# Attention on one core: the transposes of a step's two heads side by side, the gate steps between them moved to the fillings around

## The chip, the core and the metric

The kernel runs on one core of a Trainium2 chip. TensorE (PE) multiplies matrices and transposes; VectorE (DVE), ScalarE (ACT) and GpSimd (POOL) work beside it on vectors; SyncE (SP) and POOL issue most of the DMAs. TensorE's results land in PSUM, eight banks of 128 x 512 float32. The metric is device time in microseconds (us), from runs of the whole kernel.

## The reference

One block of a streaming encoder on 512 tokens of width 1024: a normalised input goes through one wide projection into two branches (gated linear attention with 4 heads, and "forgetting" attention with 8 heads), each branch is projected to 1024 channels, the two are merged by sigmoid gates that come from the same projection, then an output projection, and a gated feed-forward part with a short convolution. The part that matters here is the second branch and the gates:

```python
def fox_attention(q, k, v, log_f):              # 512 tokens, 8 heads of 64
    c = jnp.cumsum(log_f, axis=1)
    for i in range(S // Q_BLOCK):               # 4 blocks of 128 queries
        lo, hi = i * Q_BLOCK, (i + 1) * Q_BLOCK
        logits = q[lo:hi] @ k[:hi].T * scale + c[lo:hi, None] - c[None, :hi]
        p = softmax(where(causal, logits, -inf))
        outs.append(p @ v[:hi])
...
y = sigmoid(g_gla + gate_b[0]) * (o_gla @ w_gla_branch) \
    + sigmoid(g_fox + gate_b[1]) * (o_fox @ w_fox_branch)
```

## The kernel before

Every float32 matrix is split into a high and a low part, and a product is taken as three matmuls (function `mm3`, lines 314 to 316). The weights come from memory in pieces of 128 x 1024: `piece()` hands out the next one and, three pieces ahead, issues its load on SP, ScalarE's cast to the high part (L277) and VectorE's difference for the low part (L278).

The attention works on pairs of heads. There are four pairs and four query blocks, so 16 steps, in the list `steps_a`; the block `qb` of a step sees `qb + 1` blocks of 128 keys. One step has three parts, and they are written in a software pipeline over a loop index `i`:

- `logits(pair, qb)` at `i`: six matmuls into two banks `lg` (L929); per head VectorE adds the forget term `cb` and takes the minimum (L934), ScalarE takes the exponential (L939), VectorE the reciprocal of the sum (L940), ScalarE scales (L941, tile `pr`).
- `transposed(h, qb)` at `i + 1`, once for each head of the pair (h = 2 pair + 0 or 1): TensorE transposes the `qb + 1` blocks of `pr` into a bank `pt` (L951), ScalarE copies out the high part `ph` (L959), VectorE takes the low part `pl` (L960). There are two banks `pt`.
- `values(h, half)` at `i + 2`, when two query blocks are there: products of `ph` and `pl` with the values into a bank `po` (L975, L976).

Between these stand pieces of other work. `work` is a list of generators, and `fill(n)` takes n steps from it. Most of them are gates: `gate_tile` (12 in this stage, for the output gate `zr` and the merge gate `zg`) makes one 128 x 512 tile in eight steps of three matmuls in a bank `ps_mm`, fetches its weight piece before the first, and after the eighth VectorE scales the tile out of the bank (L879). The others are `prepare_k` and `prepare_q`, one step each: four transposes (L891, L902) into a bank, then ScalarE's high part (L893, L904) and VectorE's low part (L894, L905) of the keys or queries of a pair. For pairs 1 to 3 that bank is also a `ps_mm`. There are two banks `ps_mm`, taken in turn, so the next tile but one waits until a tile is read out.

The list is, in order: half of gate 0, prepare_k and prepare_q of pair 0, the rest of gate 0, gate 1, prepare_k(1), the products of gate 2, prepare_q(1), gate 2's scaling, prepare_k(2), gate 3, prepare_q(2), gate 4, prepare_k(3), gate 5, prepare_q(3), and gates 6 to 11: 104 steps, of which nine are taken ahead of the loop. How many are taken in the loop stands in the table `FILL` (L41): its row is `i % 4`, so the rows go with `qb` = 0, 1, 2, 3 of the logits, and its numbers are the fillings behind the logits, behind the first head's transposes and behind the second head's.

The instructions are written in this order, and a planner then lays out each engine's queue. It goes by priorities in the order of the source and by its own estimates of when an operand or a bank is ready; where it holds an instruction for not ready, a later one can go ahead. So the order in the trace is near that of the source, but not the same everywhere. Each queue is then run in its order.

Of the kernel before, what the change touches and what calls it, by code (L numbers as in the profile page):

```python
# [20 lines left out]
NT = T // P  # L21
# [16 lines left out]
NPB = (KB + 1) // 2  # L38
NTAIL = 5
NSPARE = 4  # L40
FILL = ((3, 2, 2), (2, 2, 2), (2, 2, 1), (2, 2, 2))  # L41
QSTEP = 8
GAHEAD = 2
NWARM = 9
# [34 lines left out]
def hybrid_kernel(ctx: ExitStack, tc, xT, xt, wp, wu, wd, wf, pp, aw2, fing, out):  # L79
# [341 lines left out]
    def fill(n=1 << 30):  # L421
        while n > 0 and work:
            try:
                next(work[0])
                n -= 1
            except StopIteration:
                work.pop(0)
# [492 lines left out]
    def logits(pair, qb):  # L920

        kh, kl, qh, ql = qk[pair]
        n = (qb + 1) * P
        q = slice(qb * P, n)
        rows = [slice(i * FD, (i + 1) * FD) for i in range(2)]
        lgs = [bank("lg") for _ in range(2)]
        for j, (a, b) in enumerate(((qh, kh), (ql, kh), (qh, kl))):
            for lg, r in zip(lgs, rows):
                mm(lg[:, :n], lhsT=a[r, q], rhs=b[r, :n], start=(j == 0), stop=(j == 2))  # L929
        for i, lg in enumerate(lgs):  # L930
            h = 2 * pair + i
            pr = fpool.tile([P, T], F32, tag="pr", name="pr", bufs=4)
            nm = fpool.tile([P, 1], F32, tag="nm", name="nm", bufs=4)
            nc.vector.tensor_tensor_reduce(  # L934
                out=pr[:, :n], in0=lg[:, :n], in1=cbs.pop((h, qb)), scale=-1.0, scalar=3e38,
                op0=ALU.add, op1=ALU.min, accum_out=nm,
            )
            rs = fpool.tile([P, 1], F32, tag="rs", name="rs", bufs=4)
            nc.scalar.activation(out=pr[:, :n], in_=pr[:, :n], func=AF.Exp, scale=-1.0, bias=nm, accum_out=rs)  # L939
            nc.vector.reciprocal(out=rs, in_=rs)  # L940
            nc.scalar.activation(out=pr[:, :n], in_=pr[:, :n], func=AF.Copy, scale=rs)  # L941
            probs[h, qb] = pr
            if h + 2 < FH:
                load_cb(h + 2, qb)

    def transposed(h, qb):
        pr = probs.pop((h, qb))
        pt = bank("pt")
        for kb in range(qb + 1):
            c = slice(kb * P, (kb + 1) * P)  # L950
            nc.tensor.transpose(pt[:, c], pr[:, c], ident)  # L951
        half, odd = qb // 2, qb % 2
        if odd == 0:
            pts[h, half] = [
                fpool.tile([P, 2 * half + 2, 2 * P], F32R, tag=f"{tag}{half}", name=tag, bufs=2) for tag in ("ph", "pl")
            ]
        ph, pl = (t[:, : qb + 1, odd * P : (odd + 1) * P] for t in pts[h, half])
        pt3 = pt.rearrange("p (a q) -> p a q", q=P)[:, : qb + 1, :]
        last_copy[:] = [nc.scalar.copy(out=ph, in_=pt3)]  # L959
        nc.vector.tensor_sub(out=pl, in0=pt3, in1=ph.bitcast(F32))  # L960
# [3 lines left out]
    def values(h, half):  # L964

        ph, pl = pts.pop((h, half))
        v2 = vs[h]
        if half == 0:
            po[h] = bank("po")
        nk = 2 * half + 2  # L970
        for kb in range(nk):
            w = v2[:, kb, :, :].rearrange("p a d -> p (a d)")
            lo = P if kb == nk - 1 else 0
            q = slice(half * 2 * P + lo, (half + 1) * 2 * P)
            mm(po[h][:, q], lhsT=w, rhs=ph[:, kb, lo:], start=(kb == 0), stop=False)  # L975
            mm(po[h][:, q], lhsT=w, rhs=pl[:, kb, lo:], start=False, stop=(kb == nk - 1))  # L976
        if half == 0:
            return

        i, pair = h % 2, h // 2  # L980
        if i == 0:
            oo[pair] = fpool.tile([P, T], F32, tag="oo", name="oo", bufs=1)

        ol = fpool.tile([P, 4, 2 * P], F32, tag="ph1", name="ol", bufs=2).rearrange("p a q -> p (a q)")[:, :T]
        nc.scalar.copy(out=ol[:FD], in_=po[h][FD:P, :])
        nc.vector.tensor_add(out=oo[pair][i * FD : (i + 1) * FD, :], in0=po[h][:FD, :], in1=ol[:FD])
        if h + 2 < FH:
            prepare_v(h + 2)

    def split_values(pair):  # L990
        nc.scalar.copy(out=oth[pair], in_=oo[pair])
        nc.vector.tensor_sub(out=otl[pair], in0=oo[pair], in1=oth[pair].bitcast(F32))

    steps_a = [(pair, qb) for pair in range(FH // 2) for qb in range(NT)]
# [9 lines left out]
    for i in range(len(steps_a) + 2):  # L1004
        last = None
        if i < len(steps_a):
            logits(*steps_a[i])
            fill(FILL[i % NT][0])
        for j in range(2):
            if 0 <= i - 1 < len(steps_a):  # L1010
                transposed(2 * steps_a[i - 1][0] + j, steps_a[i - 1][1])
                fill(FILL[i % NT][1 + j])
        if i >= 2 and steps_a[i - 2][1] % 2 == 1:
            pair, qb = steps_a[i - 2]
            for j in range(2):
                values(2 * pair + j, qb // 2)

        if i > NT and i % NT == 2:
            split_values(i // NT - 1)
# [664 lines left out]
```

## Time and profile before

| what | value |
|---|---|
| median of 3 runs | 705.51 us (704.78 to 706.0) |
| the profiled execution: time | 703.98 us |
| the profiled execution: span from first to last instruction | 702.3 us |
| TensorE busy | 693.0 us (99%) |
| VectorE busy | 551.1 us (78%) |
| ScalarE busy | 426.8 us (61%) |
| GpSimd busy | 179.3 us (26%) |
| mean granted clock of TensorE | 0.999 |
| moved by DMA | 138.20 MB |

A row of the timeline has the start in us, the duration, the engine, the line of the kernel, the operation, the output and inputs, the tile's shape, and how many neighbours of a kind are merged in it; in brackets, for how long the engine was idle before and what released it. Durations of matmuls overlap, since they are pipelined: what one costs is read from its start to the next one's. "PEld" is the loading of a matmul's weights, which runs beside the matmul before it. A row of waits has the waiting engine and line, what it waited for, the total in us, the number of times and the longest; "issue" is time in which it waited for nothing that the profile shows.

### The profile page before, as it was taken

The numbers are of one execution on the slowest core, as the hardware profiler recorded it, in microseconds if no ns is written. First come the engines' busy times: TensorE is split into PE (matmuls) and PEld (weight loads), VectorE is DVE, ScalarE is ACT, GpSimd is POOL, SyncE is SP. The second block draws the span as 40 slices with busy tenths as digits, with TensorE's granted clock in tenths as the row PEclk, the third lists the DMA queues.
The fourth block names the chain that finished last, engine by engine and source line by source line (L and its number), as shares of the span: only waits on it lengthen the run. The fifth ranks groups of instructions, "written<-read, shape, count | busy, mean of one in ns | idle before, by whom it ended". The sixth has DMA issues, their size and how long they took to land.

```text
span 702.3 us, 11231 instructions
## 1 busy us (share of the span) xinstructions
PE 693.0 (99%) x4162; PEld 601.6 (86%) x4162; DVE 551.1 (78%) x836; ACT 426.8 (61%) x690; POOL 179.3 (26%) x228
## 2 busy tenths in 40 slices
PE   8999999999999999999999999999999999999996
PEld 6887788777877888888888999999999999888885
DVE  7875887876666585677769998888988889987984
ACT  7488565667676753334484965655556566655753
POOL 7215010124231323323100133322343411000222
PEclk9999999999999999999999999999999999999999
DMA  9668478996775478977885778877777787775643
GB/s 321 267 184 276 113 239 214 310 226 150 175 172 122 105 205 219 248 178 198 195 285 120 154 182 206 189 171 185 167 185 170 196 210 227 269 211 178 194 136 120
DMA packets 44743, 138.20 MB, mean 197 GB/s; under 512 B 5240, under 2 KB 8328, under 8 KB 44560
## 3 DMA queue, kind: packets, MB, share of 16 engines
q1 hardware_dynamic: 30864, 92.85, 39.4%
q0 software_dynamic: 10656, 39.33, 31.6%
q10 hardware_dynamic: 3168, 5.31, 2.1%
q8 instruction: 33, 0.54, 0.3%
q14 instruction: 22, 0.18, 0.1%
HBM read 133.25 MB, written 27.28 MB: 229 GB/s over the span
## 4 chain that ended last, share of the span: by engine, by line
PE 90%; DVE 5%; ACT 2%; DMA 1%; issue 1%; ACTq 0%; DVEq 0%; SPq 0%
PE ps_mm L314 22%; PE ps_mm L315 21%; PE ps_mm L316 21%; PE ps_ax L315 7%; PE ps_ax L316 6%; PE ps_ax L314 6%; DVE wl L278 2%; PE ps_lg L929 2%; PE ps_pt L951 1%; PE ps_po L976 1%; PE ps_po L975 1%; DMA raw<-wsum 1%; DMA ppt<-in_pp_dram 1%; DVE xo L1274 1%; PE ps_ax L832 1%
## 5 line engine op out<-in xcount | busy, mean ns | idle before, releaser
L314 PE MATMUL ps_mm<-xh,wh 128*128 128x512 f32 (+1 forms) x312 | 109.7, 353 | 1.2 <-DVE wh L273 1.2
L277 ACT CAST wh<-rawx 128x1024 fp32r<-128x1024 f32 x75 | 76.2, 1016 | 52.8 <-PE ps_mm L315 24.1
L315 PE MATMUL ps_mm<-xl,wh 128*128 128x512 f32 (+1 forms) x312 | 106.4, 341 | 0.0
L316 PE MATMUL ps_mm<-xh,wl 128*128 128x512 f32 (+1 forms) x312 | 106.3, 342 | 0.0
L278 DVE TENSOR_TENSOR wl<-rawx,wh 128x1024 fp32r<-128x1024 f32 x75 | 88.8, 1188 | 16.4 <-ACT wh L277 16.4
L278 DVE TENSOR_TENSOR wl<-raw,wh 128x1024 fp32r<-128x1024 f32 x58 | 78.3, 1351 | 9.1 <-ACT wh L277 8.2
L277 ACT CAST wh<-raw 128x1024 fp32r<-128x1024 f32 x58 | 60.7, 1048 | 34.3 <-PE ps_mm L315 24.6
L314 PEld LDWEIGHTS ps_mm<-xh,wh 128*128 128x128 f32 x312 | 58.7, 188 | 9.6 <-issue 2.8
L316 PEld LDWEIGHTS ps_mm<-xh,wl 128*128 128x128 f32 x312 | 58.6, 188 | 7.4 <-DVE wl L274 0.4
L315 PEld LDWEIGHTS ps_mm<-xl,wh 128*128 128x128 f32 x312 | 58.8, 189 | 5.6 <-DVE xl L1183 0.2
L285 POOL DMA_DIRECT2D rawx<-in_wu_dram x30 | 26.1, 869 | 124.6 <-DVE wl L278 117.7
L278 DVE TENSOR_TENSOR wl<-rawz,wh 128x1024 fp32r<-128x1024 f32 x31 | 39.2, 1266 | 14.8 <-ACT wh L277 14.1
L314 PE MATMUL ps_mm<-xo,wh 128*128 128x256 f32 x160 | 45.4, 284 | 0.0
L315 PE MATMUL ps_mm<-xo,wh 128*128 128x256 f32 x160 | 45.3, 283 | 0.0
L316 PE MATMUL ps_mm<-xo,wl 128*128 128x256 f32 x160 | 45.3, 283 | 0.0
L314 PE MATMUL ps_mm<-xc,wh 128*128 128x256 f32 (+1 forms) x128 | 43.5, 340 | 0.0
L314 PE MATMUL ps_mm<-wh,xh 128*128 128x512 f32 x108 | 42.8, 397 | 0.1
L277 ACT CAST wh<-rawz 128x1024 fp32r<-128x1024 f32 x31 | 32.5, 1047 | 16.5 <-PE ps_mm L316 6.0
L251 POOL TENSOR_TENSOR rawx<-rawx,raw 128x256 f32<-128x256 f32 x32 | 36.7, 1175 | 22.5 <-DMA rawx<-in_wu_dram 22.5
L315 PE MATMUL ps_mm<-xc,wh 128*128 128x256 f32 (+1 forms) x128 | 42.4, 332 | 0.0
L316 PE MATMUL ps_mm<-xc,wl 128*128 128x256 f32 (+1 forms) x128 | 42.3, 331 | 0.0
L315 PE MATMUL ps_mm<-wl,xh 128*128 128x512 f32 x108 | 42.1, 390 | 0.0
(477 smaller groups left out, 1986.1 us busy)
## 6 DMA issues: line engine op xcount, KB each, us to landing
rawx<-in_wu_dram POOLq DMA_DIRECT2D x32, 512.0 KB, 6.0
rawz<-in_wp_dram SPq DMA_DIRECT2D x30, 512.0 KB, 4.3
raw<-in_wp_dram SPq DMA_DIRECT2D x22, 512.0 KB, 4.4
wsum<-in_wd_dram SPq DMA_DIRECT2D x20, 512.0 KB, 6.4
rawx<-in_wu_dram SPq DMA_DIRECT2D x20, 512.0 KB, 5.5
raw<-in_wu_dram SPq DMA_DIRECT2D x20, 512.0 KB, 4.3
rawx<-wsum SPq DMA_DIRECT2D x12, 512.0 KB, 4.4
wsum<-in_wd_dram POOLq DMA_DIRECT2D x10, 512.0 KB, 7.5
```

The lines of the kernel that those rows point to most:

```text
L251: nc.gpsimd.tensor_add(out=raws[n][:, c], in0=raws[n][:, c], in1=raws[other][:, c])
L277: nc.scalar.copy(out=hi[:, :m], in_=raw[:, :m])
L278: nc.vector.tensor_sub(out=lo[:, :m], in0=raw[:, :m], in1=hi[:, :m].bitcast(F32))
L285: added[:] = [nc.gpsimd.dma_start(raw, recipes[i][0], accum_op=ALU.add)]
L314: mm(ps, lhsT=ah, rhs=bh, start=start, stop=False, **k)
L315: mm(ps, lhsT=ah, rhs=bl, start=False, stop=False, **k)
L316: mm(ps, lhsT=al, rhs=bh, start=False, stop=stop, **k)
L832: mm(obs[par][:, c], lhsT=scs[2 * u + par][:, 2 * t2 + j, :], rhs=vg[:, 2 * u + t2, h * GDV : (h + 1) * GDV], start=(t2 == j == 0), stop=F ...
L929: mm(lg[:, :n], lhsT=a[r, q], rhs=b[r, :n], start=(j == 0), stop=(j == 2))
L951: nc.tensor.transpose(pt[:, c], pr[:, c], ident)
L975: mm(po[h][:, q], lhsT=w, rhs=ph[:, kb, lo:], start=(kb == 0), stop=False)
L976: mm(po[h][:, q], lhsT=w, rhs=pl[:, kb, lo:], start=False, stop=(kb == nk - 1))
```

## The change

Only the places at which steps of `work` are taken change. The filling between the two heads' transposes is gone; its steps are divided between the filling behind the logits and the one behind both groups of transposes. The total of each row stays (7, 6, 5, 6). At `i` = 0 there are logits and no transposes, so four steps are taken there in place of three, and from there the list stands one step further on at each of the logits; at `i` = 16, where there are only transposes, the table gives three in place of two and two.

```diff
-FILL = ((3, 2, 2), (2, 2, 2), (2, 2, 1), (2, 2, 2))
+FILL = ((4, 3), (3, 3), (3, 2), (3, 3))
...
     for i in range(len(steps_a) + 2):
         last = None
         if i < len(steps_a):
             logits(*steps_a[i])
             fill(FILL[i % NT][0])
         for j in range(2):
             if 0 <= i - 1 < len(steps_a):
                 transposed(2 * steps_a[i - 1][0] + j, steps_a[i - 1][1])
-                fill(FILL[i % NT][1 + j])
+        if 0 <= i - 1 < len(steps_a):
+            fill(FILL[i % NT][1])
         if i >= 2 and steps_a[i - 2][1] % 2 == 1:
             pair, qb = steps_a[i - 2]
             for j in range(2):
                 values(2 * pair + j, qb // 2)
```

## The prediction

> **What bounds the kernel now.** I read the page first, for the span and the busy shares of the engines; then the busy time by stretch, for the stage of the change alone; then TensorE's waits in it; then its timeline row by row.
>
> ```profile
> span 702.3 us, 11231 instructions
> PE 693.0 (99%) x4162; PEld 601.6 (86%) x4162; DVE 551.1 (78%) x836; ACT 426.8 (61%) x690; POOL 179.3 (26%) x228
> ```
>
> TensorE is busy for 693.0 of 702.3 us, far ahead of VectorE's 551.1. What the kernel loses to waits of TensorE anywhere is at most 9.3 us, so the question is how much of that lies in the attention stage. That stage runs from the first logits at 136.8 us to the last values at 235 us. The view of busy time by stretch gives it next to the start and the rest:
>
> ```profile
> core 0: us, PE busy (x) PEld busy (x) DVE busy (x) ACT busy (x) POOL busy (x), PEclk, DMA share, GB/s
> 133.00:236.00 103.00, 102.96 (x585) 82.05 (x584) 67.89 (x171) 70.55 (x167) 30.07 (x57) 1.00 0.73 175
> 0.00:8.00 8.00, 5.51 (x18) 2.76 (x19) 2.87 (x8) 4.03 (x6) 4.49 (x16) 1.00 0.76 229
> ```
>
> In the stage TensorE is busy for 102.96 of 103.00 us at a granted clock of 1.00; VectorE has work for 67.89 us and ScalarE for 70.55 us. The stage's length is therefore the sum of what TensorE issues plus small waits at its weight loads, which the view of waits lists for the same stretch:
>
> ```profile
> PEld ps_lg L929 <- issue: 2.7, 8, 0.4
> PEld ps_mm L314 <- issue: 1.9, 6, 0.4
> PEld ps_lg L929 <- DVE rs L940: 0.7, 2, 0.4
> PEld ps_mm L314 <- DVE pl L960: 0.4, 1, 0.4
> PEld ps_mm L891 <- issue: 0.2, 1, 0.2
> PEld ps_lg L929 <- DVE ql L905: 0.2, 1, 0.2
> ```
>
> These are waits of the weight loads, 6.1 us together; a running matmul hides most of each, so they bound what can be won. No row names a transpose (L951) as the waiter.
>
> **The change, part by part.** The number of gate steps per step of the loop stays at 7, 6, 5 and 6. Nothing is computed more or less: 80 transposes, 104 steps of gates and preparations, the same copies, loads and DMA issues on SP and POOL. What changes is the order. I take it in four terms.
>
> *Term 1: the switch between transposes and gate products.* Two groups of transposes per step become one group of double length. The timeline shows a group of two and one of four, with the gate matmuls around them:
>
> ```profile
> 195.74 0.39 PE L316 MATMUL ps_mm<-xh,wl 128*128 128x512 f32 x1
> 195.97 0.38 PE L951 MATMUL ps_pt<-ident,pr 128*128 128x128 f32 x2
> 196.10 0.48 PE L314 MATMUL ps_mm<-xh,wh 128*128 128x512 f32 x1
> 196.42 0.39 PE L315 MATMUL ps_mm<-xl,wh 128*128 128x512 f32 x1
> ...
> 207.83 0.40 PE L316 MATMUL ps_mm<-xc,wl 128*128 128x512 f32 x1
> 208.06 0.60 PE L951 MATMUL ps_pt<-ident,pr 128*128 128x128 f32 x4
> 208.42 0.48 PE L314 MATMUL ps_mm<-xh,wh 128*128 128x512 f32 x1
> 208.73 0.40 PE L315 MATMUL ps_mm<-xl,wh 128*128 128x512 f32 x1
> ```
>
> Start to start, a gate matmul takes 0.23 us (195.74 to 195.97). From L316 to L315 over the group of two it is 0.68 us; less two gate matmuls (0.46) the group costs 0.22 us. Over the group of four it is 0.90 less 0.46, that is 0.44 us. Twice the transposes cost twice the time, 0.11 us each, with nothing left over for the group. The first matmul behind a group does take 0.31 or 0.32 us in place of 0.23, but the group's own last transpose is shorter by as much. So joining two groups saves 0.0 us. The bounds: nothing, if the price stays 0.11 us each; and if the 0.08 us behind a group were the price of the switch, one switch less in each of some 15 steps, a gain of 1.2 us. The two rows lie on the first end and I take 0.0.
>
> [...]
>
> *Term 2: are the probabilities there?* The second head's transposes come one gate step (0.70 us) earlier, the first head's one gate step later, since the first filling grows from 3, 2, 2, 2 to 4, 3, 3, 3 steps. A step's transposes wait for the scaling on ScalarE (L941). The shortest distance is that of the last step:
>
> ```profile
> 228.01 1.34 ACT L941 ACTIVATE pr<-pr,rs 128x512 f32<-128x512 f32 x2
> 230.32 0.63 PE L951 MATMUL ps_pt<-ident,pr 128*128 128x128 f32 x4
> ```
>
> Both heads are scaled by 229.35 us, 0.97 us ahead of even the first head's transposes; the second head's would start 0.43 us behind the first's. Cost 0.0. On the other side, the second head's copy and difference come a gate step earlier, with the values that read them where they were; the first head's come a gate step later, and its values still stand behind the whole filling of the last step, or a whole step of the loop behind at the others. Cost 0.0. Each head has its own of the two pt banks and each is read out a step before it is needed, so the second group waits for no bank either. ScalarE's two copies of a step and VectorE's two differences become neighbours; their sum stays.
>
> *Term 3: one gate step ahead.* At the loop's step 0 four steps are issued in place of three, so from there the gates and the preparations (prepare_k, prepare_q) stand one step earlier against the logits. That matters only where a bank of ps_mm is needed soon after its last use. Three such places show in the trace:
>
> ```profile
> 153.08 0.39 PE L316 MATMUL ps_mm<-xc,wl 128*128 128x512 f32 x1
> 153.51 0.69 DVE L879 TENSOR_TENSOR zr<-ps_mm,rb 128x512 f32<-128x512 f32 x1 [0.73 <-PE ps_mm L316]
> 153.64 0.60 PE L902 MATMUL ps_mm<-ident,qf 128*128 128x128 f32 x4
> 154.26 0.66 PE L891 MATMUL ps_mm<-ident,kf 128*128 128x128 f32 x4
> 155.02 1.04 ACT L277 CAST wh<-rawz 128x1024 fp32r<-128x1024 f32 x1
> 155.16 0.75 DVE L905 SCALAR_TENSOR_TENSOR ql<-ps_mm,gqs,qh 128x512 fp32r<-128x512 f32 x1
> 155.97 0.33 PE L929 MATMUL ps_lg<-kh,ql 64*128 64x128 f32 x2
> ...
> 162.27 0.39 PE L929 MATMUL ps_lg<-kh,qh 64*128 64x256 f32 x2
> 162.81 0.50 PE L314 MATMUL ps_mm<-xc,wh 128*128 128x512 f32 x1
> 163.39 0.39 PE L316 MATMUL ps_mm<-xc,wl 128*128 128x512 f32 x1
> 164.19 0.36 PE L975 MATMUL ps_po<-ph,v 128*128 128x256 f32 x1
> 164.56 0.50 PE L314 MATMUL ps_mm<-xh,wh 128*128 128x512 f32 x1
> ...
> 182.22 0.39 PE L316 MATMUL ps_mm<-xc,wl 128*128 128x512 f32 x1
> 182.88 0.60 PE L951 MATMUL ps_pt<-ident,pr 128*128 128x128 f32 x4
> 183.39 0.50 PE L314 MATMUL ps_mm<-xh,wh 128*128 128x512 f32 x1
> ```
>
> From a gate's last matmul to the bank's next user it takes 1.18, 1.17 and 1.17 us (153.08 to 154.26, 163.39 to 164.56, 182.22 to 183.39): VectorE's scaling (0.69 us) and the ways there and back. Whatever TensorE has in between covers it. In the kernel before it has about 1.0 to 1.1 us there, so each place waits some 0.1 to 0.15 us (the group of four at 182.88 takes 0.51 us to the next matmul, against 0.36 at 208.06). At the first place the low half of q follows, done at 155.91: the logits at 155.97 wait for it by some 0.2 us. Together about 0.6 us.
>
> With the new order, taking 0.23 for the gate's last matmul, 0.43 for a preparation and 0.11 per transpose: at the first place six transposes and prepare_q give 0.23 + 0.64 + 0.43 = 1.30, no wait. At the second the logits of a 256-wide step (162.27 to 162.81, 0.54 us) stand ahead of prepare_q: 0.23 + 0.54 + 0.43 = 1.20, no wait. At the third the transposes move behind two gate steps: 0.23 + 0.43 = 0.66, 0.5 us short. A new place comes where pair 3's prepare_k meets gate 5: 0.23 + 0.43 + 0.43 = 1.09, 0.1 short. The low half of q took 2.33 us from prepare_q at 153.64 to its user at 155.97. Of these about 0.35 us were the two waits and some 0.2 the high part of the logits, which leaves 1.8 us of preparations and values. Now gate 3's first step stands there too, but it needs prepare_q's bank, which is free only once the low half is made: 2.33 less 1.8, 0.5 to 0.6 us short, or 0.3 to 0.4 if the high part of the logits goes first. Without any help the waits sum to 1.2 us, 0.6 more than before.
>
> There is help: the planner does not keep the source's order where it holds a product for not ready. At 164.19 a product of the values stands ahead of gate 4's, which comes ahead of it in the source. If it pulls the transposes forward at the third place likewise, that place waits 0.15 us as before and the sum is about 0.6. So term 3 lies between 0.0 and +0.6 us. I take +0.2, nearer the lower end, because the trace shows the planner doing this.
>
> *Term 4: loads and queues.* Eleven gates start a weight piece inside the stage; nine start in the same step of the loop as before, two (gates 3 and 5) one filling earlier, just ahead of the next logits. Their cast (1.04 us) and difference then stand ahead of the logits' work on ScalarE and VectorE. With 0.97 us at the tightest step and more elsewhere, 0.0; the bound is one such cast, 1.0 us. SP and POOL pass nothing.
>
> **Sum.** 0.0 + 0.0 + 0.2 + 0.0 = +0.2 us. On the profiled execution (span 702.3, time 703.98) that is 704.2 us; that execution lies 1.5 us under the median of the runs, 705.51, so the forecast of a median is 705.7 us. A measurement of this kernel tells about 0.2%, 1.4 us, from no change (its own runs spread from 704.78 to 706.0), so +0.2 is no change.
>
> **The rivals.** *The planner undoes it*: it orders by its own estimates, and could part the two groups again or pull other work between them. The time is then that of before, 705.5. For it: the reordering at 164.19. Against: nearly all groups stand in source order. Chance 0.15.
>
> *Slower: the bank of prepare_q holds TensorE.* Beside the 0.6 us of term 3, the planner puts the cast of the next piece (1.04 us, at 155.02) ahead of q's high half on ScalarE. Gate 3 and the logits behind it both need q's low half, and TensorE has nothing else ready: 0.6 + 1.04 = +1.6 us, 707.1. It decides from the point at which that cast stands in front; in the trace before it stands behind. Chance 0.18.
>
> *Slower by the clock.* A stretch of nothing but transposes grows, to 0.64 + 0.43 + 0.43 = 1.5 us at the first place. If the granted clock fell to half there, it would cost 1.5 us, 707.2. Against: in the first 8 us TensorE was busy for only 5.51 us and the clock was still 1.00. Chance 0.03. [...]
>
> *Faster: a switch has its price.* If the 0.08 us behind each group is saved (1.2 us) and all waits of term 3 go (0.6 us), it is -1.8 us, 703.7. Against: term 1's two rows. Chance 0.12.
>
> **How the numbers follow.** No change by the sum 0.52, and by the first rival 0.15: same 0.67. Slower 0.18 + 0.03 = 0.21. Faster 0.12. The range leaves out the faster rival and reaches to the slower ones: 704.3 to 707.3. The forecast's own range is 705.1 to 706.3.
>
> **What would show it.** Term 1: groups of 2, 4, 6 and 8 transposes, 0.11 us each; a shorter group says it is wrong. Term 2: no wait at L951 other than ScalarE's; otherwise the scaling was late. Term 3: gate 6's and gate 3's first matmul and pair 1's logits, waits of 0.1 to 0.6 us; over 1 us at one of them, and the slower rival has it. The clock stays at 1.00. The prediction fails if TensorE's busy time in the stage is under 102 of 103 us, or if the stage's last values end over 1.4 us earlier or later.

## The result, and the profile after

The changed kernel takes 705.74 us (median of 21 runs, 705.24 to 707.99), the kernel before in runs beside it 704.89 us (21 runs, 703.75 to 706.0). The ratio is 1.0018, with a 95% interval of 1.0011 to 1.0026. That is slower, by 0.8 us by the medians and 1.3 us by the ratio, and still inside the 0.2% that the prediction set as its bound. The times of either kernel lie in two groups some 2 us apart, for a reason that stands at the end (the pace of the first matmuls); each kernel's lower group is what its profiled execution belongs to here, 703.98 before and 705.35 after.

The page of the changed kernel, the stretch of the stage, and TensorE's waits from 133 to 237 us:

```profile
span 703.6 us, 11230 instructions
PE 693.9 (99%) x4162; PEld 602.5 (86%) x4162; DVE 553.7 (79%) x836; ACT 426.2 (61%) x690; POOL 180.3 (26%) x228
```

```profile
133.00:236.00 103.00, 101.93 (x576) 81.27 (x575) 66.50 (x170) 69.26 (x166) 29.92 (x56) 1.00 0.71 176
```

```profile
PEld ps_lg L929 <- ACT qh L904: 0.6, 1, 0.6
PEld ps_mm L314 <- DVE zg L879: 0.6, 1, 0.6
PEld ps_mm L314 <- DVE ql L905: 0.4, 1, 0.4
PEld ps_pt L951 <- DVE pl L960: 0.2, 1, 0.2
```

The span is 1.3 us longer, TensorE's busy time in the same 103 us is 101.93 in place of 102.96, at the same clock of 1.00. Four waits are new by name: on the high half of pair 1's queries, on their low half at a gate's first product, on the scaling of a gate, and a small one of the transposes on a low part. No other part of the kernel can have taken much: from the first logits (L929) to the first of the last sixteen value products (L975) it is 136.78 to 233.30, 96.52 us, before, and 136.91 to 234.87, 97.96 us, after. This stretch, 1.44 us longer, is the measure of all that follows; a trace gives it to a tenth of a microsecond (97.97 us in E4's trace of the same kernel), far more sharply than the runs' times (705.24 to 707.99 us).

The timeline of the changed kernel at the two main places, selected rows of ScalarE and VectorE among TensorE's:

```profile
153.83 0.60 PE L902 MATMUL ps_mm<-ident,qf 128*128 128x128 f32 x4
154.13 0.46 ACT L959 CAST ph<-ps_pt 128x384 fp32r<-128x384 f32 x1
154.49 0.72 ACT L941 ACTIVATE pr<-pr,rs 128x512 f32<-128x512 f32 x1
155.12 0.46 ACT L959 CAST ph<-ps_pt 128x384 fp32r<-128x384 f32 x1
155.48 0.69 ACT L904 ACTIVATE qh<-ps_mm,gqs 128x512 fp32r<-128x512 f32 x1
156.20 0.75 DVE L905 SCALAR_TENSOR_TENSOR ql<-ps_mm,gqs,qh 128x512 fp32r<-128x512 f32 x1
156.22 0.33 PE L929 MATMUL ps_lg<-kh,qh 64*128 64x128 f32 x2 [0.47 <-ACT qh L904]
157.00 0.50 PE L314 MATMUL ps_mm<-xh,wh 128*128 128x512 f32 x1 [0.20 <-DVE ql L905]
...
183.25 0.39 PE L316 MATMUL ps_mm<-xc,wl 128*128 128x512 f32 x1
183.91 0.60 PE L951 MATMUL ps_pt<-ident,pr 128*128 128x128 f32 x4
184.06 0.16 DVE L940 RECIPROCAL rs<-rs 128x1 f32<-128x1 f32 x1 [0.35 <-ACT pr L939]
184.14 0.67 DVE L879 TENSOR_TENSOR zg<-ps_mm,rb 128x512 f32<-128x512 f32 x1
184.87 0.50 PE L314 MATMUL ps_mm<-xh,wh 128*128 128x512 f32 x1 [0.35 <-DVE zg L879]
```

At the first place the queries of pair 1 are transposed at 153.83, but ScalarE makes their high half only at 155.48: a head's copy, the scaling of the next step's probabilities and the other head's copy stand ahead of it. In the kernel before, both copies stood ahead of it as well, but both scalings had gone ahead of the copies:

```profile
152.49 1.32 ACT L941 ACTIVATE pr<-pr,rs 128x512 f32<-128x512 f32 x2
153.71 0.83 ACT L959 CAST ph<-ps_pt 128x384 fp32r<-128x384 f32 x2
154.44 0.69 ACT L904 ACTIVATE qh<-ps_mm,gqs 128x512 fp32r<-128x512 f32 x1
```

There the high half started 0.80 us behind prepare_q (153.64); now it is 1.65 us. Gate 3 takes prepare_q's bank, and so waits until the low half has been made from it: it starts at 157.00, 3.17 us behind prepare_q. In the kernel before, the first to wait for the low half were the logits, 2.33 us behind prepare_q. At the second place gate 5's last matmul starts at 183.25 and its scaling at 184.14: VectorE stands at a reciprocal that waits for ScalarE's exponential, with the scaling behind it. Gate 6 starts 1.62 us behind that matmul; before it was 1.17.

### The profile page after: what moved, and what is told of

The parts are those of the page before. It is cut to its first block, busy times and chain, and to the rows that moved or that the text cites. A ratio compares the mean times of both kernels' runs of the same rounds, so it can differ in the third digit from the quotient of the medians.

```text
span 703.6 us, 11230 instructions
## 1 busy us (share of the span) xinstructions
PE 693.9 (99%) x4162; PEld 602.5 (86%) x4162; DVE 553.7 (79%) x836; ACT 426.2 (61%) x690; POOL 180.3 (26%) x228
## 4 chain that ended last, share of the span: by engine, by line
PE 84%; ACT 6%; DVE 6%; DMA 2%; issue 1%; ACTq 0%; DVEq 0%; SPq 0%
PE ps_mm L314 20%; PE ps_mm L315 19%; PE ps_mm L316 19%; PE ps_ax L315 7%; PE ps_ax L316 6%; PE ps_ax L314 6%; ACT pr L939 2%; DVE wl L278 1%; DMA rawx<-wsum 1%; ACT pr L941 1%; ACT wh L277 1%; PE ps_pt L951 1%; PE ps_lg L929 1%; PE ps_po L976 1%; DMA cb<-nct 1%
## 5 line engine op out<-in xcount | busy, mean ns | idle before, releaser
L314 PE MATMUL ps_mm<-xh,wh 128*128 128x512 f32 (+1 forms) x312 | 109.4, 352 | 1.4 <-DVE wh L273 0.8
L315 PE MATMUL ps_mm<-xl,wh 128*128 128x512 f32 (+1 forms) x312 | 106.5, 342 | 0.0
L316 PE MATMUL ps_mm<-xh,wl 128*128 128x512 f32 (+1 forms) x312 | 106.4, 342 | 0.0
L314 PEld LDWEIGHTS ps_mm<-xh,wh 128*128 128x128 f32 x312 | 59.2, 190 | 11.3 <-issue 2.5
L316 PEld LDWEIGHTS ps_mm<-xh,wl 128*128 128x128 f32 x312 | 59.1, 190 | 7.2 <-DVE wl L274 0.2
L315 PEld LDWEIGHTS ps_mm<-xl,wh 128*128 128x128 f32 x312 | 59.3, 190 | 5.8 <-DVE xl L1184 0.2
L314 PE MATMUL ps_mm<-xo,wh 128*128 128x256 f32 x160 | 45.5, 284 | 0.0
L316 PE MATMUL ps_mm<-xo,wl 128*128 128x256 f32 x160 | 45.4, 283 | 0.0
L315 PE MATMUL ps_mm<-xo,wh 128*128 128x256 f32 x160 | 45.3, 283 | 0.0
L314 PE MATMUL ps_mm<-xc,wh 128*128 128x256 f32 (+1 forms) x128 | 43.0, 336 | 0.0
L314 PE MATMUL ps_mm<-wh,xh 128*128 128x512 f32 x108 | 42.8, 398 | 0.1
L315 PE MATMUL ps_mm<-xc,wh 128*128 128x256 f32 (+1 forms) x128 | 42.5, 332 | 0.0
L316 PE MATMUL ps_mm<-xc,wl 128*128 128x256 f32 (+1 forms) x128 | 42.3, 331 | 0.0
L315 PE MATMUL ps_mm<-wl,xh 128*128 128x512 f32 x108 | 42.2, 390 | 0.0
```

The lines of the kernel that those rows point to most:

```text
L314: mm(ps, lhsT=ah, rhs=bh, start=start, stop=False, **k)
L315: mm(ps, lhsT=ah, rhs=bl, start=False, stop=False, **k)
L316: mm(ps, lhsT=al, rhs=bh, start=False, stop=stop, **k)
```

## The experiments

In each fence the line numbers are those of that run's own kernel. E5, E6 and E9 were run once each, so they are read by the stretch in their trace and not by their times. Two theories stood against each other. P: grouping costs nothing, the loss is at a few places where a preparation or a gate meets an operand or a bank that is not ready. G: the grouping itself costs, by the burst of copies and differences.

**E1, e1_group_only.** Grouped as in the changed kernel, without the step ahead.

```diff
-FILL = ((4, 3), (3, 3), (3, 2), (3, 3))
+FILL = ((3, 4), (3, 3), (3, 2), (3, 3))
```

> The transposes of both heads stand together as in the changed kernel, but FILL's first row is (3, 4) in place of (4, 3): the gates are not a step ahead of the logits. Measure: the stretch from the first logits to the first of the last 16 value products, 96.5 us before and 98.0 us after. Theory P (places: what costs is where a preparation or a gate now meets a bank or an operand that is not ready, for pair 1's queries and gate 6): 96.3 to 96.8 us, ratio to before 0.9995 to 1.0005, gate 6 waits under 0.2 us. Rival G (the grouping itself costs, since ScalarE's and VectorE's work of the two heads comes in one burst): 97.6 to 98.2 us, ratio 1.0015 to 1.002.

Measured: stretch 136.75 to 233.13, 96.38 us; ratio 0.9997 (0.9986 to 1.0009). P holds, G falls: with all transposes grouped the stage is 0.14 us shorter than before.

**E2, e2_shift_only.** The kernel before, with its transposes apart, and the step ahead.

```diff
-FILL = ((3, 2, 2), (2, 2, 2), (2, 2, 1), (2, 2, 2))
+FILL = ((4, 1, 2), (2, 2, 2), (2, 2, 1), (2, 2, 2))
```

> The transposes stay apart as before, but FILL's first row is (4, 1, 2) in place of (3, 2, 2): the gates are one step ahead of the logits, as in the changed kernel. Same stretch. Theory P: 97.0 to 97.9 us, ratio 1.0005 to 1.0015, with waits of 0.3 to 0.6 us at pair 1's first logits or gate 3 and at gate 6. Rival G: 96.4 to 96.7 us, ratio 1.000.

Measured: stretch 136.81 to 234.73, 97.92 us, at the upper end of P's range; ratio 1.0014 (1.0003 to 1.0025). The shift alone brings nearly all of the loss, with not one group joined. The places are not quite P's: the weight loads wait 0.5 us at gate 3 and 0.3 at gate 6, but pair 1's last logits and gate 5 take 0.5 us more as well (3.18 us for the work that took 2.67 before), where the prediction had only 0.1. So the shift alone and the changed kernel lose about the same, but not all at the same places.

**E3, e3_two_places.** The changed kernel with another division at two steps of the loop (AT overrides FILL's row at these i).

```diff
+AT = {3: (4, 2), 8: (2, 5)}
-            fill(FILL[i % NT][0])
+            fill(AT.get(i, FILL[i % NT])[0])
...
-            fill(FILL[i % NT][1])
+            fill(AT.get(i, FILL[i % NT])[1])
```

> The changed kernel with another division at two steps of the loop only: i = 3 takes (4, 2) in place of (3, 3), so that prepare_q of pair 1 stands ahead of the transposes; i = 8 takes (2, 5) in place of (4, 3), so that all eight transposes stand between prepare_q of pair 3 and gate 6. Theory P: both waits go (1.1 us and 0.5 us down to 0.2 or less each), the stretch is 96.4 to 96.9 us, ratio to before 0.9995 to 1.0005. Rival G: 97.6 to 98.0 us, ratio 1.0015 to 1.002.

Measured: stretch 138.84 to 235.60, 96.76 us; ratio 1.0003 (0.9991 to 1.0014). Two steps of seventeen, divided otherwise, win 1.2 of the 1.44 us back. Gate 6's wait fell to 0.2 us; of the wait at pair 1, 0.5 us stayed, at gate 3's first matmul, where P had 0.2 or less.

**E4, e4_after_again.** The changed kernel itself beside these.

> The changed kernel itself, beside the others on the same chip: stretch 97.9 to 98.1 us, ratio to before 1.001 to 1.0025 under both theories.

Measured: stretch 136.87 to 234.84, 97.97 us; ratio 1.0025 (1.0013 to 1.0036).

**E5, e5_scaling_first.** The changed kernel with gate 5's scaling ahead of that step's reciprocals on VectorE. In logits, for pair 2 and block 0, the reciprocal and the scaling of pr go into a list, and behind the filling:

```diff
             fill(FILL[i % NT][0])
+            while late:
+                with tc.issue_after(last_scaling[0].ins):
+                    late.pop(0)()
```

> The changed kernel, but at the loop's step 8 the reciprocals of the step's two heads (and the scalings behind them) are written behind that filling and held behind gate 5's scaling on VectorE; TensorE's order stays. Theory V (gate 6 waits since VectorE, in its fixed order, stands at a reciprocal that waits for ScalarE's exponential, with gate 5's scaling behind it): gate 5's scaling starts under 0.5 us behind gate 5's last matmul in place of 0.9 us, gate 6's wait falls from 0.5 us to 0.1 to 0.2, the stretch from the first logits to the last 16 values from 98.0 to 97.5 to 97.7 us. Rival B (the way from the last matmul to the bank's next user is simply longer there): wait and stretch stay at 0.5 and 98.0 us.

The timeline of E5 at that place:

```profile
183.20 0.39 PE L316 MATMUL ps_mm<-xc,wl 128*128 128x512 f32 x1
183.67 0.69 DVE L879 TENSOR_TENSOR zg<-ps_mm,rb 128x512 f32<-128x512 f32 x1
184.27 0.38 DVE L942 RECIPROCAL rs<-rs 128x1 f32<-128x1 f32 x2
184.41 0.50 PE L314 MATMUL ps_mm<-xh,wh 128*128 128x512 f32 x1
```

The scaling starts 0.47 us behind the last matmul in place of 0.89, and gate 6 1.21 us behind it in place of 1.62; the stretch is 136.89 to 234.38, 97.49 us. Theory V holds: what had lengthened the way from the matmul to the bank's next user was VectorE's order.

**E6, e6_copies_late.** The changed kernel with the heads' copies and differences of the loop's step 3 behind the halves of pair 1's queries.

```diff
+        if (h, qb) in ((0, 2), (1, 2)):
+            late.append(copies)
...
+            while late:
+                with tc.issue_after(last_q[0].ins), tc.issue_after(last_q[1].ins):
+                    late.pop(0)()
```

> The changed kernel, but at the loop's step 3 the copies and differences of the transposed probabilities (ScalarE's two of 0.46 us, VectorE's two of 0.56 us) are written behind that step's filling and held behind the high and low half of pair 1's queries; TensorE's order as the planner then makes it. Theory S (pair 1's logits and gate 3 wait because the queries' high half stands behind the heads' copies in ScalarE's order): the queries' high half starts 0.4 to 0.6 us earlier against prepare_q's transposes (1.65 us in the changed kernel), the waits there fall from 1.1 us to 0.4 to 0.7, the stretch from 98.0 to 97.3 to 97.6 us. Rival B (only the distance on TensorE counts): 97.9 to 98.1 us.

Measured: both theories missed. The stretch is 136.63 to 236.66, 100.03 us, and the waits at the place 1.4 us in place of 1.0. ScalarE's rows there:

```profile
153.85 1.03 ACT L277 CAST wh<-rawz 128x1024 fp32r<-128x1024 f32 x1
154.78 0.72 ACT L944 ACTIVATE pr<-pr,rs 128x512 f32<-128x512 f32 x1
155.41 0.66 ACT L906 ACTIVATE qh<-ps_mm,gqs 128x512 fp32r<-128x512 f32 x1
```

The planner put the cast of a weight piece (1.03 us) in the place that the copies had left, and the queries' half came no earlier. The rest of the loss is the clock, in the view of stretches (the column behind POOL is the granted clock):

```profile
156.00:158.00 2.00, 1.42 (x9) 0.87 (x9) 2.00 (x5) 1.29 (x4) 0.85 (x2) 1.00 0.92 289
158.00:160.00 2.00, 2.00 (x9) 1.58 (x8) 1.22 (x7) 1.29 (x6) 1.48 (x4) 0.67 0.63 232
160.00:162.00 2.00, 2.00 (x6) 1.54 (x5) 0.00 (x0) 0.22 (x1) 0.28 (x1) 0.50 0.66 88
162.00:164.00 2.00, 2.00 (x14) 1.73 (x14) 0.13 (x1) 0.75 (x2) 0.81 (x2) 0.98 0.95 182
```

Behind the 1.4 us of waits TensorE ran at half clock for some 3.4 us (0.33 of 2 us, 0.5 of 2 us and 0.02 of 2 us are missing, 1.7 us together, at half rate 3.4 us), which cost 1.7 us more.

**E7, e7_group_and_early_q.** E1 with prepare_q of pair 1 ahead of the six transposes.

```diff
+AT = {3: (5, 1)}
```

> The kernel e1_group_only (grouped transposes, first row (3, 4)), with (5, 1) in place of (3, 3) at i = 3, so that prepare_q of pair 1 stands ahead of the six transposes. Theory P: e1's two waits at that place (0.2 and 0.4 us) go, the stretch falls from its 96.4 to 95.7 to 96.0 us, ratio to before 0.9985 to 0.9995 (about 0.7 us faster, at the edge of what can be told). Rival G as far as it is left (six transposes close to ScalarE's other work cost elsewhere): 96.3 us or more, ratio 0.9995 to 1.0005.

Measured: a miss for P. The stretch is 136.89 to 234.12, 97.23 us, ratio 1.0024 (1.0010 to 1.0038). It was not G's bursts either: the same cast again, and on VectorE its difference.

```profile
154.06 1.03 ACT L277 CAST wh<-rawz 128x1024 fp32r<-128x1024 f32 x1
155.00 0.68 ACT L904 ACTIVATE qh<-ps_mm,gqs 128x512 fp32r<-128x512 f32 x1
155.18 1.22 DVE L278 TENSOR_TENSOR wl<-rawz,wh 128x1024 fp32r<-128x1024 f32 x1 [1.24 <-ACT wh L277]
156.32 0.74 DVE L905 SCALAR_TENSOR_TENSOR ql<-ps_mm,gqs,qh 128x512 fp32r<-128x512 f32 x1
```

The low half is done at 157.06 and the logits wait 1.5 us. The median (706.29) lies further up than the stretch says, and the granted clocks of the runs suggest why: five of the twelve, from 706.48 to 708.07 us, have a mean of 0.995, as the run of E6 has, and every run of the other versions whose clock is on record has 0.997 to 0.999. So the clock very likely fell in these five as in E6, though no trace of them shows where; in the profiled one, at 0.999, it did not.

**E8, e8_early_q_cast_behind.** E7 with that cast and difference held behind the halves.

```diff
+        if pair == 1:
+            hold[:] = [high, low]          # in prepare_q: the two halves' instructions
...
+            with ExitStack() as es:         # in split_next, around cast and difference
+                for q in hold:
+                    es.enter_context(tc.issue_after(q.ins))
```

> The kernel e7_group_and_early_q with one order more: the next weight piece's cast on ScalarE and its difference on VectorE are held behind the high and the low half of pair 1's queries. Theory C (e7's 1.5 us of waits at pair 1's logits were the cast of 1.03 us and the difference of 1.22 us that the planner set in front of the two halves): both waits go under 0.2 us, the stretch from the first logits to the last 16 values falls from 97.2 to 95.7 to 96.0 us, ratio to before 0.9985 to 0.9995. Rival B (prepare_q ahead of the transposes is bad by itself): 96.8 us or more, ratio above 1.000.

```profile
154.17 0.67 ACT L910 ACTIVATE qh<-ps_mm,gqs 128x512 fp32r<-128x512 f32 x1
154.87 0.75 DVE L911 SCALAR_TENSOR_TENSOR ql<-ps_mm,gqs,qh 128x512 fp32r<-128x512 f32 x1 [0.82 <-ACT qh L910]
155.94 1.07 ACT L282 CAST wh<-rawz 128x1024 fp32r<-128x1024 f32 x1
```

Measured: the low half is done at 155.62, no wait is left there, the stretch is 136.99 to 232.75, 95.76 us. The ratio is 0.9989 (0.9979 to 0.9998), 703.27 us against 704.11: the one version whose whole interval lies below 1, its ratio by a tenth of a per cent. Theory C holds. Whether the kernel before, with its transposes apart, would win as much from the same order of cast and halves was not run.

**E9, e9_copies_late_cast_behind.** E6 with the cast and difference held likewise.

> The kernel e6_copies_late with the same order more: the next piece's cast and difference behind the queries' halves, and the heads' copies and differences too. Theory C and S together (what stands ahead of the queries' high half in ScalarE's order sets the wait at pair 1): the high half starts about 0.9 us behind prepare_q's first transpose in place of 1.65 us in the changed kernel and 1.86 in e6, the waits at pair 1's logits and gate 3 are 0.4 to 0.7 us in place of 1.1 and 1.4, the clock does not fall, the stretch is 97.3 to 97.6 us against 98.0. Rival B: 97.9 us or more.

Measured: the high half starts 0.98 us behind prepare_q's transposes (156.49 against 155.51), the clock stays, the stretch is 138.59 to 236.16, 97.57 us. The wait is 0.7 us, at the upper end of what was expected: the scaling of pr still stands ahead of the half. With the changed kernel's table of fillings, then, another order of the copies, the cast and their differences on ScalarE and VectorE wins 0.4 us.

## Why the prediction was right or wrong

The median came out at 705.74 where 705.7 was forecast, and the change is under 0.2%, but that the two medians agree so closely is luck: the forecast was +0.2 us on a median of 705.51 from three runs, and the kernel before measured 704.89 in the larger set. The loss is 1.44 us in the stage, seven times the forecast. By two of the signs that the prediction itself set, it failed: TensorE's busy time is 101.93 us, under 102, and the stage's last value product starts at 236.58 in place of 235.01 us, 1.57 us later, over 1.4. Its third sign, a single wait of over 1 us, did not come; the two at pair 1 are 0.6 and 0.4 us. By its steps:

*Term 1 was right.* Groups of four and eight in the changed kernel:

```profile
210.64 0.39 PE L316 MATMUL ps_mm<-xh,wl 128*128 128x512 f32 x1
210.87 1.03 PE L951 MATMUL ps_pt<-ident,pr 128*128 128x128 f32 x8
211.66 0.48 PE L314 MATMUL ps_mm<-xh,wh 128*128 128x512 f32 x1
211.97 0.40 PE L315 MATMUL ps_mm<-xl,wh 128*128 128x512 f32 x1
...
223.74 0.60 PE L951 MATMUL ps_pt<-ident,pr 128*128 128x128 f32 x4
224.10 0.48 PE L314 MATMUL ps_mm<-xc,wh 128*128 128x512 f32 x1
224.41 0.39 PE L315 MATMUL ps_mm<-xc,wh 128*128 128x512 f32 x1
```

From L316 to L315 the group of eight takes 1.33 us, less 0.46 it is 0.87, 0.11 us each; the group of four has the same 0.36 us to L314 and 0.31 behind it as in the kernel before. A switch has no price of its own, the faster rival falls, and E1 says it for the whole stage: 96.38 us against 96.52.

*Term 2 was right for the probabilities and wrong for the bank.* No transpose waits for the scaling of pr. But "each is read out a step before it is needed" fails once, at the last step:

```profile
231.92 1.02 DVE L960 TENSOR_TENSOR pl<-ps_pt,ph 128x384 fp32r<-128x384 f32 x2 [1.42 <-ACT ph L959]
232.53 1.12 PE L951 MATMUL ps_pt<-ident,pr 128*128 128x128 f32 x8
```

The two differences of the step before, late behind ScalarE's exponentials and scalings, still read the banks, and the eight transposes wait 0.2 us. E1, without the step ahead, has no wait there.

*Term 3 named the two places and was mis-sized.* It set 0.0 to +0.6 us and took +0.2. The way at pair 1's place grew by 0.84 us (2.33 to 3.17, some 0.1 of it a transpose that now stands in it) and the one at gate 6 by 0.45 us (1.17 to 1.62). The step ahead as a whole cost 1.4 us by itself (E2) and 1.6 us on top of the grouping (from E1 to the changed kernel). The step that failed is the taking of a way's length for a constant: "1.18, 1.17 and 1.17 us" from a gate's last matmul to the bank's next user, and "2.33 us" from prepare_q to the low half's user. Both hold an order of ScalarE and VectorE. With the logits one gate step nearer, a reciprocal stood in front at gate 6, and a scaling with the second head's copy behind it at pair 1. E5 shows the first with the order put right: 1.21 us. For pair 1 it is shown in part: in E9, with the changed kernel's fillings, gate 3 starts 2.48 us behind prepare_q in place of 3.17 (157.99 against 155.51), with 0.7 us of waiting left; E8, where no wait is left, has another order on TensorE too. The upper end "without any help" was therefore no upper end. The planner did pull transposes forward at gate 6, as the prediction had it (four at 183.91), and it helped less than counted for this reason. That the new order would end two waits of the kernel before was right (neither place waits now), and worth some 0.1 to 0.15 us each by its own figures.

*Term 4* stands at 0.0 for the changed kernel, whose cast at this place is behind the halves. *The slower rival* had the right mechanism and its stated turning point, the cast in front of the queries' high half: it did not happen in the changed kernel, it happened in E6 and E7, where the waits were 1.4 and 1.5 us against its 1.6.

*The clock rival* was refuted in its form: at the first place there is nothing but transposes from 153.18 to 154.63 us, as it had counted, and the clock stays at 1.00. The row set against it was half empty, though, as the last section shows, and in E6 the clock did fall in this stage, behind 1.4 us of waits. *That the planner undoes the change* fell too; apart from one transpose pulled ahead of gate 3 and four pulled ahead of gate 6, the groups stand.

## What to carry to other kernels

Here, with TensorE busy 99% of the time, moving its work about won little by itself (0.14 us in E1, with all transposes grouped); it lost at the few places where the next use of a bank or operand follows soon (1.4 us in E2), and these can be listed from the order before any run. The latency of such a place was not a constant read from one row (1.17 us at gate 6 before, 1.62 us after): it holds the order of the engines in between, so list what else becomes ready there at that time, casts of later weights among it (1.03 us in E6 and E7), and pin the order of what the next product needs. Compare stretches between two events of TensorE, in traces, when an effect is below the scatter of the times.

## What the runs showed of the hardware

The clock fell to half in E6 behind only 1.4 us of waiting, in two pieces (0.81 and 0.60 us) with products between, and came back after 3.4 us; while the column read 0.50, a 128x512 matmul came every 0.43 us in place of 0.23. E7's profiled execution waited 1.5 us, in two pieces as well (0.26 and 1.21 us), and kept its clock: behind the waits its matmuls come every 0.23 us. What decides between the two stays open.

The two groups of times come, as far as the traces show, from the start. In E3's profiled execution (705.93 us, its upper group) the first products run at about half the pace for longer than in the kernel before:

```profile
9.18 0.63 PE L315 MATMUL ps_mm<-xl,wh 128*128 128x512 f32 x1
9.61 0.63 PE L316 MATMUL ps_mm<-xh,wl 128*128 128x512 f32 x1
10.04 0.59 PE L314 MATMUL ps_mm<-xh,wh 128*128 128x512 f32 x1
10.46 0.40 PE L315 MATMUL ps_mm<-xl,wh 128*128 128x512 f32 x1
```

```profile
6.70 0.63 PE L315 MATMUL ps_mm<-xl,wh 128*128 128x512 f32 x2
7.17 0.66 PE L316 MATMUL ps_mm<-xh,wl 128*128 128x512 f32 x2
7.67 0.40 PE L315 MATMUL ps_mm<-xl,wh 128*128 128x512 f32 x1
7.90 0.39 PE L316 MATMUL ps_mm<-xh,wl 128*128 128x512 f32 x1
```

The first fence is E3, with 0.43 us from matmul to matmul until 10.46 us, as in E6 at the column's 0.50; the second is the kernel before, at 0.23 to 0.25 us from 6.70 us on. E3's first logits come at 138.84 us against 136.78, which is all of the 2 us. E9 has them at 138.59 us, so its start was most likely of the same kind; the other nine traces have them between 136.63 and 136.99 us. The column of the granted clock says 1.00 for these first microseconds all the same (0 to 4 and 4 to 8 us, in E3 as in the kernel before). The trace has no record of the clock before 10.45 us in E3 and before 3.98 us in the kernel before, and the column reads 1.00 where there is none. So the row on which the prediction rested its answer to the clock rival ("busy for only 5.51 us and the clock was still 1.00") bears it for only half of its 8 us: at the start, the distance between matmuls is the better witness.
